# High parts of the recurrence's 16 weight tiles by a casting transfer on GpSimd's queue

## The chip, the cores and the metric

The kernel runs on one core of a Trainium2 chip. The metric is the device time of one execution in microseconds. The median of three runs before the change is 1561.8 us (1561.55 to 1561.82).

## What is computed

A decoder trunk of two layers over 512 positions of width 1024, all in float32. Each layer adds half a feed-forward block, a token mixer, and half a feed-forward block again, each behind a root-mean-square norm. The mixer of layer 0 is a recurrence (RG-LRU behind a causal convolution of width 4), that of layer 1 a chunked spatial gating. The change touches the first product of the recurrence:

```python
def recurrent_mixer(x, w_in, conv_w, conv_b, gate_a_w, gate_a_b, gate_x_w, gate_x_b, lam, w_out):
    y, r = jnp.split(x @ w_in, 2, axis=-1)
    y = jax.nn.gelu(y)
    r = causal_depthwise_conv(r, conv_w, conv_b)
    h = rg_lru(r, gate_a_w, gate_a_b, gate_x_w, gate_x_b, lam)
    return (y * h) @ w_out
```

Here w_in is 1024 x 2048: its right half gives r, its left half y.

## The kernel before

**Splitting.** TensorE multiplies in a rounded 32-bit format (float32r). To keep float32's accuracy, each factor is split in two: hi is the value rounded to float32r, lo is the value minus hi. A product is then three matmuls: high by high, high by low, low by high (mm3, L242). For a weight tile this is done in Sub.split (L189): ScalarE copies the loaded tile raw into whi with the rounding (L202), and VectorE subtracts whi from raw into wlo (L203). All ScalarE activations carry the line of the helper act (L114), all two-tensor operations of VectorE that of tt (L105), and those with a scalar that of stt (L111). So the profile's lines tell helpers, and the tile names tell the work.

**Weight tiles.** A tile is 128 x 1024 float32, 512 KB. SyncE loads it into one of 10 buffers called raw (L153). Some tiles of other stages get a second weight added by GpSimd's accumulating load (L156). The pool wp has 4 buffers for whi and 4 for wlo (L77). There is no such loading for the recurrence's input products beyond the plain load.

**The order of the work** is written out by hand. The kernel is a list of products (subs), and the loop at L1760 goes through it: for product i it first issues the splits up to product i + 3 (SPLIT_AHEAD), then work that was hung on this place by name ("mid", "rest"), then loads, then the matmuls of product i, then what takes their result from PSUM ("end", "late"). Every engine takes its own instructions in the order of issue, and a wait for another engine or for a transfer stops all that is behind it on the same engine.

**The recurrence's input products** (recurrent, mk, L1338) are 16 tiles of 1024 rows by 128 columns, loaded in rows of 512 bytes, each for 24 matmuls. The first eight, r0 to r7, give r; the next eight, y0 to y7, give y. The first four run in two halves over the positions, because the second half of the normed input is ready later: r0 to r3 over the first 256 positions, then a0 to a3 over the other 256 with the same whi and wlo. The others run over all 512 positions at once. Between r2 and r3 TensorE transposes the second half of the normed input (L700).

When the result for block c of r is there, ScalarE takes it from PSUM and VectorE adds the other three taps of the convolution (taps, L1227: three stt into rc). In the next step rc is split (hi on ScalarE, lo<-rc on VectorE), and then TensorE forms two gate products from it (gate, L1231: six matmuls, the second and the fifth of which read lo). In VectorE's order the subtraction for the tile three products ahead stands before that lo<-rc, since splits of weights come first in each step. From block 0 on there stands also a product (pr) between them, once the gates' results come back.

**The stage before** is the output product of the first feed-forward block. Its last four products run just before r0, in 12 matmuls each. In the last of them two splits are called ahead of time and one after it (L837 to L840). In this region VectorE also splits the gates' weights (gw) and updates the sum x, then scales the rows that the transposes before r3 take (xn).

Of the kernel before, what the change touches and what calls it, by code (L numbers as in the profile page):

```python
# [9 lines left out]
F32R = mybir.dt.float32r  # L10
U16 = mybir.dt.uint16
AF = mybir.ActivationFunctionType
ALU = mybir.AluOpType

P = 128
# [55 lines left out]
def trunk(ctx: ExitStack, tc: tile.TileContext, a: dict, out: bass.AP):  # L71
    nc = tc.nc
# [4 lines left out]
    wp = ctx.enter_context(tc.tile_pool(name="wp", bufs=4))  # L77
# [7 lines left out]
    def nm(s):  # L85
        uid[0] += 1
        return f"{s}_{uid[0]}"

    def slot(dt=F32, name="s"):
        return sp.tile([P, T], dt, tag="s", name=nm(name))  # L90
# [10 lines left out]
    def f32(t):  # L101
        return t.bitcast(F32)

    def tt(o, x, y, op):
        nc.vector.tensor_tensor(out=o, in0=x, in1=y, op=op)  # L105
# [7 lines left out]
    def act(o, x, f, **k):  # L113
        nc.scalar.activation(out=o, in_=x, func=f, **k)  # L114

    def split(src):

        w = src.shape[-1]
        hi, lo = slot(F32R, "hi")[:, :w], slot(F32R, "lo")[:, :w]
        act(hi, src, AF.Copy)  # L120
        tt(lo, src, f32(hi), ALU.subtract)
        return hi, lo
# [6 lines left out]
    class Raw:  # L129


        halves = False

        def __init__(self, src, shape, plus=None, wait=2):
            self.src, self.shape, self.plus, self.wait, self.uses, self.done = src, shape, plus, wait, 0, 0
# [19 lines left out]
        def add(self, src):  # L155
            nc.gpsimd.dma_start(out=self.v, in_=src, accum_op=ALU.add)  # L156
# [6 lines left out]
    def run_pending():  # L163
        while pending and pending[0][0] <= now[0]:
            raw = pending.pop(0)[1]
            raw.add(raw.plus)
            raw.plus = None

    class Sub:
# [4 lines left out]
        def __init__(self, raw, mm, post=None, tile=None, then=None, tile_then=None):  # L174
            self.raw, self.mm, self.post, self.tile, self.then = raw, mm, post, tile, then
            self.tile_then = tile_then
            self.hi, self.at = None, (raw.turn(), tile and tile.turn())

        def add(self):
            if self.tile is None or (self.raw.done, self.tile.done) != self.at:  # L180
# [5 lines left out]
            self.tile.used()  # L186
            self.tile = None

        def split(self, between=None):  # L189

            if self.hi is not None:
                return
            self.add()
            src = self.raw.v
            assert self.tile is None and self.raw.plus is None and self.raw.done == self.at[0]
            _, k, c = src.shape
            self.hi = wp.tile([P, 1024], F32R, tag="whi", name=nm("whi"))[:, : k * c].rearrange(
                "p (k c) -> p k c", k=k)
            self.lo = wp.tile([P, 1024], F32R, tag="wlo", name=nm("wlo"))[:, : k * c].rearrange(
                "p (k c) -> p k c", k=k)  # L200
            for q in ((slice(0, 1), slice(1, 2)) if self.raw.halves else (slice(0, k),)):
                act(self.hi[:, q, :], src[:, q, :], AF.Copy)  # L202
                tt(self.lo[:, q, :], src[:, q, :], f32(self.hi[:, q, :]), ALU.subtract)  # L203
                if between is not None and q.start == 0:
                    between()
            if self.then is not None:
                self.raw.add(self.then)
            self.raw.used()

    class Again:  # L210
# [3 lines left out]
            self.sub, self.mm, self.post = sub, lambda _: mm(sub), post  # L214

        def add(self):
            pass

        def split(self):
# [4 lines left out]
    def raw_of(src, shape, *plus):  # L224
        raws.append(Raw(src, shape, *plus))
        return raws[-1]

    subs = []
# [9 lines left out]
    def run(phase):  # L238
        for fn in hooks.pop((now[0], phase), []):
            fn()  # L240

    def mm3(ps, wh, wl, xh, xl, start, stop):  # L242
        nc.tensor.matmul(ps, wh, xh, start=start, stop=False)  # L243
        nc.tensor.matmul(ps, wh, xl, start=False, stop=False)  # L244
        nc.tensor.matmul(ps, wl, xh, start=False, stop=stop)  # L245
# [24 lines left out]
    class Group:  # L270
# [81 lines left out]
        def parts(self, name, last=False):  # L352
            if name in self.gain:
                self.direct(name, self.f[name], [g for g, _ in self.gain[name]])
            else:
                self.hl[name] = split(self.f[name])
            if last:
                del self.f[name]
# [703 lines left out]
    class FinalNorm:  # L1062
# [90 lines left out]
        def keep(self, scale):  # L1153

            n = now[0]

            def parts():
                self.x = split(xt(1, 1))
                self.eye = cp.tile([P, P], F32R, tag="eye", name="eye")
                act(self.eye, ident, AF.Copy, scale=1.0 / scale)  # L1160

            def gain():
                self.gain[2] = slot(name="fg")
                act(self.gain[2], self.gain[1], AF.Copy, scale=scale)

            hook(n + 2, "mid", parts)
            hook(n + 3, "mid", gain)
# [30 lines left out]
    def recurrent(w_in, w_out, norm):  # L1198
# [10 lines left out]
        def split_gate(name, q):  # L1209
            gates[name, q] = split(gates[name, q])  # L1210
# [127 lines left out]
        def mk(c0, post, halves):  # L1338

            raw = raw_of(w_in[:, c0 : c0 + P].rearrange("(k p) c -> p k c", p=P), [P, KD, P])  # L1340
            st = {}

            def mm_of(t):
                def mm(s):
                    if not st:
                        st[0] = (aux if c0 < 2 * P else bank)("r")
                    for k in KORDER:
                        xh, xl = (z[:, t] for z in S.z[k])
                        mm3(st[0][:, t], s.hi[:, k, :], s.lo[:, k, :], xh, xl, k == KORDER[0], k == KORDER[-1])
                return mm  # L1350

            last = lambda: post(st[0])
            if not halves:
                subs.append(Sub(raw, mm_of(slice(0, T)), last))
                return []
            subs.append(Sub(raw, mm_of(slice(0, H))))
            return [Again(subs[-1], mm_of(slice(H, T)), last)]

        again = []
        for c in range(4):  # L1360
            again += mk(D + c * P, lambda ps, c=c: r_post(c, ps), True)
        subs.extend(again)
        for c in range(4, KD):
            mk(D + c * P, lambda ps, c=c: r_post(c, ps), False)
        assert len(subs) == y0
        for c in range(KD):
            mk(c * P, lambda ps, c=c: y_post(c, ps), False)
# [251 lines left out]
    def load_more(n=len(raws)):  # L1619
        nonlocal loaded  # L1620
        while loaded < n and len(live) < RAW_BUFS:
            raws[loaded].load()
            loaded += 1
# [136 lines left out]
    for i, s in enumerate(subs):  # L1760
        now[0] = i
        run_pending()
        run("pre")
        upto = ahead.get(i, i + SPLIT_AHEAD)
        for q in range(i, min(upto + 1, len(subs))):
            if i >= 2 and q == upto and q + 1 < len(subs):
                subs[q + 1].add()
            subs[q].split()
        run("mid")
        run("rest")  # L1770
        load_more()
        s.mm(s)
        run("end")
        if s.post is not None:
            s.post()
        run("late")
# [26 lines left out]
```

## Time and profile before

| | us |
|---|---|
| runs, median (lowest to highest) | 1561.8 (1561.55 to 1561.82) |
| span of the profiled execution, first to last instruction | 1559.5 |
| ScalarE's copies raw to whi, whole kernel: 567, mean 1.001 | 564.4 |
| VectorE's subtractions to wlo, whole kernel: 567, mean 1.153 | 651.9 |
| GpSimd busy | 245.3 |

The page gives the span of the profiled execution and no time of its own beside it; the runs' median is 2.3 us above the span. The granted clock of TensorE is 0.999 on the mean. Windows and timelines below count from the span's start. In the timeline a line has the start, the length, the engine, the source line, the operation, out<-in, and in brackets the idle time before it with what ended it. In the windows, the recurrence's input products stand from 329 to 430 us.

A matmul's length in the timeline (0.39 us for 512 columns) overlaps the next one's: starts are 0.227 us apart for 512 columns and 0.12 for 256.

### The profile page before, as it was taken

Reading aid. Unit: us, or ns where it says so; the run is one execution under the profiler, and the core shown is the slowest. Engines: PE = TensorE matmul, PEld = TensorE weight load, DVE = VectorE, ACT = ScalarE, POOL = GpSimd, SP = SyncE. Lnnn points to the kernel's source line nnn. Section 1 sums busy time; section 2 is a strip of 40 time slices with the busy share of each in tenths; the row PEclk is TensorE's granted clock in tenths of the full one; section 3 lists DMA queues with packets and bytes.
Section 4 is the critical chain, followed back from the end, with each engine's and each line's share of the span. In section 5 each row is a group of like instructions: output and inputs, shape, how many; then the busy total and the mean of one; then the engine's idle time right before and its main releaser. Section 6 shows DMA issues by size and latency. Waiting matters only on the chain.

```text
span 1559.5 us, 21004 instructions
## 1 busy us (share of the span) xinstructions
PE 1551.9 (100%) x7293; PEld 1318.4 (85%) x7293; DVE 1309.5 (84%) x1776; ACT 1188.7 (76%) x1777; POOL 245.3 (16%) x220
## 2 busy tenths in 40 slices
PE   9999999999999999999999999999999999999998
PEld 7888888898888998888889988888888889888886
DVE  6977789888999777789897877798879997777998
ACT  7877787668778868796877787867787877778856
POOL 2111112300020111112211111122211111111220
PEclk9999999999999999999999999999999999999999
DMA  9888899953395988899977888989878859898994
GB/s 315 189 189 196 186 217 229 228 137 109 103 230 137 191 199 198 189 232 224 244 179 183 188 203 185 227 227 238 224 191 219 203 138 216 197 212 177 241 235 138
DMA packets 268763, 310.53 MB, mean 199 GB/s; under 512 B 111232, under 2 KB 149232, under 8 KB 268656
## 3 DMA queue, kind: packets, MB, share of 16 engines
q1 hardware_dynamic: 214368, 210.02, 46.4%
q0 software_dynamic: 52496, 97.33, 37.0%
q10 hardware_dynamic: 1792, 1.84, 0.4%
q8 instruction: 57, 0.93, 0.2%
q14 instruction: 50, 0.41, 0.1%
HBM read 282.39 MB, written 2.10 MB: 182 GB/s over the span
## 4 chain that ended last, share of the span: by engine, by line
PE 98%; DVE 1%; DMA 0%; ACT 0%; issue 0%; SPq 0%; DVEq 0%
PE A L479 15%; PE A L478 15%; PE A L480 15%; PE C L480 8%; PE C L479 8%; PE C L478 8%; PE B L479 4%; PE B L480 4%; PE B L478 4%; PE r L243 2%; PE r L244 2%; PE r L245 2%; PE Q L480 2%; PE Q L479 2%; PE Q L478 2%; PE p L958 1%
## 5 line engine op out<-in xcount | busy, mean ns | idle before, releaser
L105 DVE TENSOR_TENSOR wlo<-raw,whi 128x1024 fp32r<-128x1024 f32 (+2 forms) x567 | 651.9, 1153 | 208.3 <-ACT whi L114 206.7
L114 ACT ACTIVATE whi<-raw 128x1024 fp32r<-128x1024 f32 (+2 forms) x567 | 564.4, 1001 | 239.0 <-DVE raw L105 93.1
L478 PE MATMUL A<-whi,hi 128*128 128x512 f32 (+1 forms) x1104 | 421.0, 381 | 0.0
L479 PE MATMUL A<-whi,lo 128*128 128x512 f32 (+1 forms) x1104 | 419.3, 380 | 0.1
L480 PE MATMUL A<-wlo,hi 128*128 128x512 f32 (+1 forms) x1104 | 419.3, 380 | 0.0
L478 PEld LDWEIGHTS A<-whi,hi 128*128 128x128 f32 x1104 | 207.3, 188 | 35.9 <-ACT c L114 1.0
L480 PEld LDWEIGHTS A<-wlo,hi 128*128 128x128 f32 x1104 | 207.2, 188 | 35.6
L479 PEld LDWEIGHTS A<-whi,lo 128*128 128x128 f32 x1104 | 207.3, 188 | 35.4 <-DVE lo L105 0.5
L156 POOL DMA_DIRECT2D raw<-in_ffn_w_in_dram x100 | 120.7, 1207 | 710.1 <-DVE raw L105 322.8
L478 PE MATMUL C<-whi,hi 128*128 128x512 f32 (+1 forms) x608 | 231.4, 381 | 0.0
L479 PE MATMUL C<-whi,lo 128*128 128x512 f32 (+1 forms) x608 | 231.3, 380 | 0.0
L480 PE MATMUL C<-wlo,hi 128*128 128x512 f32 (+1 forms) x608 | 231.3, 380 | 0.0
L156 POOL DMA_DIRECT2D raw<-in_ffn_w_out_dram x73 | 83.8, 1194 | 319.1 <-DVE wlo L105 199.2
L105 DVE TENSOR_TENSOR raw<-raw,raw 128x1024 f32<-128x1024 f32 (+1 forms) x113 | 131.0, 1159 | 1.1
L479 PEld LDWEIGHTS C<-whi,lo 128*128 128x128 f32 x608 | 114.1, 188 | 20.1 <-DVE lo L105 0.2
L478 PEld LDWEIGHTS C<-whi,hi 128*128 128x128 f32 x608 | 114.2, 188 | 19.9
L480 PEld LDWEIGHTS C<-wlo,hi 128*128 128x128 f32 x608 | 114.1, 188 | 19.9
L105 DVE TENSOR_TENSOR lo<-a,hi 128x512 fp32r<-128x512 f32 (+1 forms) x184 | 119.7, 658 | 1.4 <-ACT hi L114 1.3
L114 ACT ACTIVATE hi<-a 128x512 fp32r<-128x512 f32 (+1 forms) x184 | 107.8, 596 | 14.5 <-DVE a L105 12.8
L114 ACT ACTIVATE c<-A 128x512 f32<-128x512 f32 (+1 forms) x150 | 81.9, 567 | 46.5 <-PE A L480 46.1
L479 PE MATMUL B<-whi,lo 128*128 128x512 f32 (+1 forms) x304 | 115.7, 381 | 0.2 <-DVE lo L111 0.2
L478 PE MATMUL B<-whi,hi 128*128 128x512 f32 (+1 forms) x304 | 115.7, 381 | 0.0
(189 smaller groups left out, 1964.5 us busy)
## 6 DMA issues: line engine op xcount, KB each, us to landing
raw<-in_ffn_w_in_dram SPq DMA_DIRECT2D x143, 512.0 KB, 5.6
raw<-in_ffn_w_out_dram SPq DMA_DIRECT2D x98, 512.0 KB, 5.7
raw<-in_ffn_w_in_dram POOLq DMA_DIRECT2D x76, 512.0 KB, 7.7
raw<-in_ffn_w_out_dram POOLq DMA_DIRECT2D x58, 512.0 KB, 7.6
raw<-in_ffn_w_in_dram SPq DMA_DIRECT2D x48, 384.0 KB, 4.2
raw<-in_sg_w_in_dram SPq DMA_DIRECT2D x20, 512.0 KB, 7.0
raw<-in_ffn_w_in_dram POOLq DMA_DIRECT2D x24, 384.0 KB, 6.3
raw<-in_rec_w_in_dram SPq DMA_DIRECT2D x16, 512.0 KB, 5.4
```

What stands on the lines that cost most here:

```text
L105: nc.vector.tensor_tensor(out=o, in0=x, in1=y, op=op)
L114: nc.scalar.activation(out=o, in_=x, func=f, **k)
L156: nc.gpsimd.dma_start(out=self.v, in_=src, accum_op=ALU.add)
L243: nc.tensor.matmul(ps, wh, xh, start=start, stop=False)
L244: nc.tensor.matmul(ps, wh, xl, start=False, stop=False)
L245: nc.tensor.matmul(ps, wl, xh, start=False, stop=stop)
L478: nc.tensor.matmul(ps, zh, wh, start=fresh and i == 0, stop=False, **k)
L479: nc.tensor.matmul(ps, zl, wh, start=False, stop=False, **k)
L480: nc.tensor.matmul(ps, zh, wl, start=False, stop=end, **k)
L958: nc.tensor.matmul(bank_of(half, s), z, (sub.lo if m == 2 else sub.hi)[:, q, :], start=left[2] == "2" and (h, q, m) == (0, 0, 0), stop=lef ...
```

## The change

The 16 tiles of mk are marked (raw.cast = True). For a marked tile, whi is no longer written by ScalarE's copy: a second transfer reads the same weights from DRAM again and writes them into whi, converting float32 to float32r on the way. It is issued by GpSimd's queue. The loop issues it for the product one beyond the splits, that is four ahead, after the splits of this step and ahead of this product's matmuls. VectorE's subtraction stays where it was. The plain load of raw stays as well, since the subtraction reads it. If the transfer was not issued ahead, split issues it itself.

```diff
@@ class Raw
-        halves = False
+        halves = cast = False
@@ class Sub
+        def cast(self):
+
+            if not self.raw.cast or self.hi is not None:
+                return
+            _, k, c = self.raw.v.shape
+            self.hi = wp.tile([P, 1024], F32R, tag="whi", name=nm("whi"))[:, : k * c].rearrange(
+                "p (k c) -> p k c", k=k)
+            nc.gpsimd.dma_start(out=self.hi, in_=self.raw.src)
+
         def split(self, between=None):
 
+            if self.raw.cast and self.lo is None:
+                self.cast()
+                _, k, c = self.raw.v.shape
+                self.lo = wp.tile([P, 1024], F32R, tag="wlo", name=nm("wlo"))[:, : k * c].rearrange(
+                    "p (k c) -> p k c", k=k)
+                tt(self.lo, self.raw.v, f32(self.hi), ALU.subtract)
+                self.raw.used()
             if self.hi is not None:
                 return
@@ def mk
             raw = raw_of(w_in[:, c0 : c0 + P].rearrange("(k p) c -> p k c", p=P), [P, KD, P])
+            raw.cast = True
@@ the loop over subs
             subs[q].split()
+        if upto + 1 < len(subs):
+            subs[upto + 1].cast()
         run("mid")
```

More of the change, by code (lines that the diff above doesn't have):

```diff
@@ L176, in __init__ @@
             self.tile_then = tile_then
-            self.hi, self.at = None, (raw.turn(), tile and tile.turn())
+            self.hi, self.lo, self.at = None, None, (raw.turn(), tile and tile.turn())
         def add(self):
@@ L216, in add, with cast @@
         def add(self):
+            pass
+        def cast(self):
             pass
```

## The prediction

> **What bounds the kernel now.** I read the page's first and fourth part, then TensorE's waits over the whole span, then the windows of the recurrence's input products.
>
> ```profile
> span 1559.5 us, 21004 instructions
> PE 1551.9 (100%) x7293; PEld 1318.4 (85%) x7293; DVE 1309.5 (84%) x1776; ACT 1188.7 (76%) x1777; POOL 245.3 (16%) x220
> PE 98%; DVE 1%; DMA 0%; ACT 0%; issue 0%; SPq 0%; DVEq 0%
> ```
>
> ```profile
> PE warm L1640 <- DVE warm L1635: 1.3, 1, 1.3
> PE B L479 <- DVE lo L111: 0.2, 1, 0.2
> ```
>
> ```profile
> 345.13:392.00 46.87, 46.87 (x243) 40.11 (x241) 39.99 (x53) 38.66 (x54) 2.41 (x2) 1.00 0.37 98
> 392.00:430.00 38.00, 38.00 (x169) 31.50 (x168) 36.53 (x52) 27.18 (x38) 3.12 (x3) 1.00 0.36 102
> ```
>
> The reader is to see three things. TensorE bounds everything: 1551.9 of 1559.5 us, 98% of the chain that ended last, and in the whole span it waited 1.5 us for others. In the two windows (length; busy us of PE, PEld, DVE, ACT, POOL; clock; DMA share; GB/s) it has no idle time at all. VectorE is nearly as full there, 85% and then 96%. So nothing that becomes cheaper on ScalarE can bring time, and whatever makes TensorE wait is paid in full, because no later stage has slack on TensorE to win it back.
>
> **What goes.** ScalarE's copies raw to whi of the 16 tiles, each like the one at 346.01 below, 1.05 us: 16.8 us of ScalarE. They lie beside TensorE's matmuls, so they are worth 0 to the end. VectorE's subtraction no longer waits for ScalarE.
>
> **What comes.** Sixteen casting transfers on GpSimd's queue, 512 KB each, and a new wait. The whi ring has 4 buffers. When the transfer for the product four ahead is called for, all four belong to this product and the next three, so the transfer waits until TensorE has ended this product. Before, the copy waited for the same buffer, but took 1.05 us. Now the subtraction that makes wlo, in its old place in VectorE's order, waits for release, issue and landing. Behind it on VectorE stand the low parts of the convolved rows (lo<-rc), and TensorE's gate products wait for those.
>
> **How long the transfer takes** (D, issue to landing). No casting transfer is in this trace, so it is bounded by neighbours of the same 512 KB, all in the stretch after 348 us. The first fence has GpSimd's accumulating loads issued at 387.64 and at 367.08 (last column: us to landing), the second their issues, the third SyncE's plain loads of the very same weights in rows of 512 bytes.
>
> ```profile
> raw<-in_rec_w_out_dram POOLq DMA_DIRECT2D x1, 512.0 KB, 6.1
> raw<-in_rec_w_out_dram POOLq DMA_DIRECT2D x1, 512.0 KB, 8.2
> ```
>
> ```profile
> 367.08 1.21 POOL L156 DMA_DIRECT2D raw<-in_rec_w_out_dram  x1 [59.97 <-DMA raw<-in_rec_w_out_dram]
> 387.64 1.20 POOL L156 DMA_DIRECT2D raw<-in_rec_w_out_dram  x1 [19.35 <-DMA raw<-in_rec_w_out_dram]
> ```
>
> ```profile
> DMA to landing us min/median/max: 3.9/3.9/3.9
> ```
>
> ```profile
> 420.08 1.23 DVE L105 TENSOR_TENSOR wlo<-raw,whi 128x1024 fp32r<-128x1024 f32 x1 [0.26 <-ACT whi L114]
> 421.62 1.20 POOL L156 DMA_DIRECT2D raw<-in_rec_w_out_dram  x1 [32.78 <-DVE wlo L105]
> ```
>
> ```profile
> L156 POOL DMA_DIRECT2D raw<-in_rec_w_out_dram x8 | 9.7, 1268 | 132.2 <-DMA raw<-in_rec_w_out_dram 79.3 <-DVE wlo L105 52.8
> L1653 POOL DMA_DIRECT2D stage<-in_rec_lambda_dram x1 | 0.5, 499 | 4.0 <-DMA raw<-in_ffn_w_in_dram 4.0
> q0 software_dynamic: 52496, 97.33, 37.0%
> ```
>
> (The last line, the software queue's packets, MB and share of 16 engines, serves a rival below.) From the end of the releasing instruction (420.08 + 1.23) to the issue on GpSimd go 0.3 us. Low end of D: 3.9, if a cast is as quick as SyncE's plain load. A cast does not read its destination as an accumulation does, which speaks for less than 6.1. But it has rows of 512 bytes: 1024 where an accumulating load of 2048-byte rows has 256. GpSimd's instruction takes 0.50 us for 4 KB in 8 rows and 1.27 for 256 rows, 0.003 us a row; 1024 rows would then take about 3.6 us (an estimate), which speaks for more. I take D = 6.1, the calm accumulating load: same queue, same bytes, same stretch. High end within reason: 8.2 to 9.
>
> The Trainium skill speaks against this size: "DMA: Bandwidth & Descriptors", section "Anatomy of one DMA — SWDGE (gpsimd) path", fits a transfer on this path as 2.0 us plus its bytes at 436 GB/s, by which 512 KB would land in 3.2 us. The trace does not agree for its own transfers on that queue (6.1 and 8.2 us); by the rule the sum below would be 0, which is the first rival.
>
> **Where TensorE will wait.** A product's matmuls follow each other without a gap, so its end is the next one's first matmul plus about 0.16 us. Names: r0 to r7 and y0 to y7 are the 16 tiles in order, a0 to a3 the second halves of r0 to r3.
>
> Place 1, gate(0). TensorE's and VectorE's rows, and ScalarE's copy:
>
> ```profile
> 345.13 0.28 PE L243 MATMUL r<-zh,whi 128*128 128x256 f32 x1
> 351.12 0.40 PE L244 MATMUL gate<-lo,hi 128*128 128x512 f32 x1
> ```
>
> ```profile
> 346.01 1.05 ACT L114 ACTIVATE whi<-raw 128x1024 fp32r<-128x1024 f32 x1
> ```
>
> ```profile
> 346.14 2.32 DVE L111 SCALAR_TENSOR_TENSOR rc<-r,vec,rc 128x509 f32<-128x509 f32 x3 [2.78 <-ACT rc L114]
> 348.38 1.22 DVE L105 TENSOR_TENSOR wlo<-raw,whi 128x1024 fp32r<-128x1024 f32 x1
> 349.51 0.68 DVE L105 TENSOR_TENSOR lo<-rc,hi 128x512 fp32r<-128x512 f32 x1
> ```
>
> 345.13 is a1's first matmul, so a0 and with it r0's whi buffer are done at 345.3. r4's transfer is issued at 345.6 and lands at 351.7. VectorE, ready at 348.4, stands until then; subtraction 1.13 (start to start), lo<-rc 0.69: 353.5. The second gate matmul needs that lo and would have run at 351.12. **Wait 2.4 us.** In general the wait is 0.46 + D + 1.13 + 0.69 less the 5.99 us between those two matmuls: it opens at D = 3.7.
>
> Places 2 and 3, gate(4) and gate(7). Here a product of 0.60 (pr<-rc,g) stands between subtraction and lo:
>
> ```profile
> 362.08 0.39 PE L243 MATMUL gate<-hi,hi 128*128 128x512 f32 x1
> 370.46 0.39 PE L244 MATMUL gate<-lo,hi 128*128 128x512 f32 x1
> 383.84 0.39 PE L243 MATMUL r<-zh,whi 128*128 128x512 f32 x1
> 390.86 0.39 PE L244 MATMUL gate<-lo,hi 128*128 128x512 f32 x1
> ```
>
> ```profile
> 387.62 1.21 DVE L105 TENSOR_TENSOR wlo<-raw,whi 128x1024 fp32r<-128x1024 f32 x1
> 388.75 0.69 DVE L105 TENSOR_TENSOR pr<-rc,g 128x512 f32<-128x512 f32 x1
> 389.35 0.68 DVE L105 TENSOR_TENSOR lo<-rc,hi 128x512 fp32r<-128x512 f32 x1
> ```
>
> From the buffer's release to a low part in use go 0.46 + 6.1 + 1.13 + 0.60 + 0.69 = 8.98 us. For gate(4) the product r4 ends before 362.08 and the low part is wanted at 370.46, 8.38 later: **wait 0.6**. For gate(7) r7 ends before 383.84 and it is wanted at 390.86, 7.02 later: **wait 2.0**. They open at D = 5.5 and 4.1. Gates 1, 2, 3, 5 and 6 have a longer way or gain it from the wait before them: 0.
>
> Place 4, r2. The first tiles' transfers wait for the FFN's last four output products, 12 matmuls and 2.72 us each; the second of them ends before 323.56, so the others before 320.84, 326.28 and 329.00:
>
> ```profile
> 323.56 0.39 PE L478 MATMUL A<-whi,hi 128*128 128x512 f32 x1
> 335.00 0.28 PE L245 MATMUL r<-zh,wlo 128*128 128x256 f32 x1
> 339.30 0.36 PE L243 MATMUL r<-zh,whi 128*128 128x256 f32 x1
> ```
>
> ```profile
> 325.07 0.68 DVE L105 TENSOR_TENSOR lo<-gw,hi 128x512 fp32r<-128x512 f32 x1
> 325.67 1.22 DVE L105 TENSOR_TENSOR wlo<-raw,whi 128x1024 fp32r<-128x1024 f32 x1
> 326.81 0.68 DVE L105 TENSOR_TENSOR lo<-gw,hi 128x512 fp32r<-128x512 f32 x1
> 327.41 2.48 DVE L111 SCALAR_TENSOR_TENSOR x<-A,x 128x512 f32<-128x512 f32 x4
> 329.80 1.27 DVE L111 SCALAR_TENSOR_TENSOR x<-Q,x 128x512 f32<-128x512 f32 x2
> 331.00 1.21 DVE L105 TENSOR_TENSOR wlo<-raw,whi 128x1024 fp32r<-128x1024 f32 x1
> ```
>
> r1's tile lands at 323.56 + 0.46 + 6.1 = 330.1, and VectorE, which began that subtraction at 325.67, now stands for it. Then 1.14 + 0.60 + 2.4 + 1.2 and r2's subtraction 1.13 with 0.1 to be seen: 336.7. r2's first matmul on wlo ran at 335.00. **Wait 1.7**, opening at D = 4.4. r0's own low part is there at 328.5 and TensorE wants it at 329.2: 0, but at D above 6.8 it too is late.
>
> **Sum:** 2.4 + 0.6 + 2.0 + 1.7 = 6.7 us; 1559.5 + 6.7 = 1566.2 in the profiled execution's own span. The runs' median of 1561.8 lies 2.3 above the span, what lies around it, and I keep that: **1568.5 us**.
>
> **Costed at nothing.** After gate(7) VectorE is about as late as TensorE, so the y products find their wlo in time. r3's transfer is only called for inside its own split; it is due at 335.6 and read by TensorE from 339.30. The DMA engines are 36 to 37% busy, and 16 more transfers of 512 KB hide there; without that cover D rises, which the range holds. On GpSimd's queue two of the gates' memsets now come behind r2's transfer, issued at 326.7; the gate weights loaded into them are split only after r3. Two of the accumulating loads stand between the transfers, but wait for loads that land before the next buffer is free: 0, and if one blocked, D would grow for one tile. PSUM: if r4's bank is the one that the third convolution's rows free, r4 waits up to 0.8 more; taken as 0, held in the range.
>
> **The rivals.**
> 1. Not slower: the transfer lands fast. Place: the same four waits; point of decision: D. At D = 5.1 they are 1.4 + 0 + 1.0 + 0.7 = 3.1 us; at 3.9 only gate(0)'s 0.2 are left. Time 1562 to 1564.9. For it: SyncE's plain load of the same rows at 3.9. Against: every load of GpSimd's in that stretch.
> 2. Much slower: a packet of the cast costs what an accumulating one does. 37.0% of 1559.5 us on 16 engines over 52496 packets is 0.176 us each; 64 rows for each engine make 11.3 us, D about 12, and the four waits and r0's make some 30 us: 1592. At D = 9 it is 18 us, 1580. For it: four times the rows. Against: a cast reads nothing back.
> 3. The change does not do what it says: the transfer copies bits and rounds nothing. Then its time is the forecast's still, and only the values differ. The Trainium skill, same page, section "SWDGE vs HWDGE vs iDMA", says that a float32r destination always casts and only from GpSimd; no run here shows it, and it moves no term.
> 4. Faster: ScalarE's 16.8 us would have to shorten a wait of TensorE's, and it has 1.5 us of those in the whole span, none in this stage.
>
> **How the numbers follow.** Forecast (D from 5.1 to 9, 1565 to 1580): 0.62. Rival 1: 0.22. Rival 2 above D = 9: 0.12. Rival 4: 0.04. Rival 3 has no time of its own. About 0.2%, 3.1 us, is what a measurement of this kernel can tell from no change. Slower 0.62 + 0.12 = 0.74, same 0.22, faster 0.04. Range: 1562 (D under 4) to 1582 (D near 10), which leaves out some 1 in 10 on either side.
>
> **What would show it.** In the changed trace the transfer's time to landing is the one number to read first. Right: TensorE's waits name VectorE's lo at L105 at the second matmul of gate(0) and gate(7), some 2 us each, and VectorE's name the DMA of whi. Wrong: TensorE without idle time between 329 and 392, or waits at wlo inside the y products, or a transfer issued long before or after the end of the product whose buffer it takes.

## The result: 10 us slower, and the profile after

| | before | after |
|---|---|---|
| runs, median (lowest to highest), us | 1561.81 (1561.55 to 1563.87) | 1571.87 (1570.97 to 1572.77) |
| span of the profiled execution, us | 1559.5 | 1571.0 |
| profiled execution's own time, us | not given | 1572.77 |

The ratio is 1.0063, with a 95% interval from 1.0051 to 1.0075. The forecast was +6.7 us and 1568.5; measured is +10.1 us by the medians and +11.5 by the two spans, which compare one execution each. Of the four executions after, two took 1572.7 us at a mean granted clock of 0.998, the profiled one among them, and two 1571.0 us at 0.999; so what the views below show of a half clock may hold for the first pair alone. In the changed kernel the lines behind the new code have moved: mm3 by 19 to L262 to L264, the warm-up by 20 to L1660. The casting transfer is L196.

The same views after, page first, then TensorE's waits (line, whom it waited for, us in total, times, longest):

```profile
span 1571.0 us, 21027 instructions
PE 1555.5 (99%) x7293; PEld 1319.1 (84%) x7293; DVE 1309.6 (83%) x1776; ACT 1173.7 (75%) x1761; POOL 257.5 (16%) x236
...
q0 software_dynamic: 69136, 105.72, 39.6%
...
PE 93%; issue 3%; DVE 2%; DMA 1%; ACT 1%; POOL 0%; SPq 0%; POOLq 0%; DVEq 0%; ACTq 0%
```

```profile
PE gate L263 <- DVE lo L105: 3.8, 4, 1.4
PE r L264 <- DVE wlo L105: 3.0, 2, 2.2
PE warm L1660 <- DVE warm L1655: 1.3, 1, 1.3
PE r L262 <- DMA whi<-in_rec_w_in_dram: 1.0, 1, 1.0
```

ScalarE has its 16 instructions less and 15.0 us less work (1188.7 to 1173.7), and the time does not show it. TensorE, which waited 1.5 us in the whole span before, now waits 7.8 us more in three new kinds: at gate products for VectorE's lo, inside r products for wlo, and once for a transfer itself. Each of them in TensorE's timeline (in brackets the wait and its releaser):

```profile
333.33 0.36 PE L262 MATMUL r<-zh,whi 128*128 128x256 f32 x1 [1.03 <-DMA whi<-in_rec_w_in_dram]
334.67 0.39 PE L264 MATMUL r<-zh,wlo 128*128 128x256 f32 x1 [0.86 <-DVE wlo L105]
339.99 0.58 PE L264 MATMUL r<-zh,wlo 128*128 128x256 f32 x1 [2.18 <-DVE wlo L105]
...
359.25 0.50 PE L263 MATMUL gate<-lo,hi 128*128 128x512 f32 x1 [1.45 <-DVE lo L105]
379.38 0.50 PE L263 MATMUL gate<-lo,hi 128*128 128x512 f32 x1 [0.36 <-DVE lo L105]
387.20 0.50 PE L263 MATMUL gate<-lo,hi 128*128 128x512 f32 x1 [0.73 <-DVE lo L105]
402.32 0.50 PE L263 MATMUL gate<-lo,hi 128*128 128x512 f32 x1 [1.22 <-DVE lo L105]
```

In order these are r1 (twice), r2, gate(0), gate(4), gate(5) and gate(7). The cause of one of them, gate(0), on GpSimd and VectorE:

```profile
351.99 0.88 POOL L196 DMA_DIRECT2D whi<-in_rec_w_in_dram  x1 [21.62 <-PE r L264]
```

```profile
352.73 2.31 DVE L111 SCALAR_TENSOR_TENSOR rc<-r,vec,rc 128x509 f32<-128x509 f32 x3 [2.84 <-ACT rc L114]
357.37 1.23 DVE L105 TENSOR_TENSOR wlo<-raw,whi 128x1024 fp32r<-128x1024 f32 x1 [2.33 <-DMA whi<-in_rec_w_in_dram]
358.51 0.69 DVE L105 TENSOR_TENSOR lo<-rc,hi 128x512 fp32r<-128x512 f32 x1
```

The reader is to see the chain: GpSimd waits for the end of a product (PE r L264) and issues; VectorE has its convolution done at 355.0, stands 2.33 us for the landing, subtracts, and only then makes the lo that TensorE has been waiting for. The subtraction's own tile, r4, is not wanted before 364.87. What is late is only what stands behind it.

Landing times of the casting transfers, from the list of DMA issues (all 16 with their median, then single ones from short windows: r1, r4, y0 and y1), and their spread from the view of the line that issues them:

```profile
whi<-in_rec_w_in_dram POOLq DMA_DIRECT2D x16, 512.0 KB, 5.6
whi<-in_rec_w_in_dram POOLq DMA_DIRECT2D x1, 512.0 KB, 9.1
whi<-in_rec_w_in_dram POOLq DMA_DIRECT2D x1, 512.0 KB, 5.4
whi<-in_rec_w_in_dram POOLq DMA_DIRECT2D x1, 512.0 KB, 6.1
whi<-in_rec_w_in_dram POOLq DMA_DIRECT2D x1, 512.0 KB, 7.1
```

```profile
DMA to landing us min/median/max: 4.5/5.6/9.1
```

And two windows of the changed kernel (length; busy of PE, PEld, DVE, ACT, POOL; granted clock; DMA share; GB/s), then the first of them before the change:

```profile
324.00:333.50 9.50, 8.47 (x49) 7.36 (x49) 2.21 (x4) 0.05 (x1) 3.63 (x5) 1.00 1.27 250
340.20:343.20 3.00, 3.00 (x15) 3.00 (x16) 2.56 (x10) 0.93 (x2) 0.00 (x0) 0.50 0.66 177
```

```profile
324.00:333.50 9.50, 9.50 (x61) 8.62 (x60) 9.09 (x18) 5.52 (x13) 0.00 (x0) 1.00 0.76 197
```

While the transfers of r1 to r3 fly, the DMA engines' share is 1.27 (transfers overlap in it) where it was 0.76, and VectorE works 2.21 of 9.5 us where it worked 9.09. Right behind the wait at r2 the granted clock is 0.50 for three microseconds.

### The profile page after: what moved, and what is told of

The parts are those of the page before. It is cut to its first block, busy times and chain, and to the rows that moved or that the text cites. A ratio compares the mean times of both kernels' runs of the same rounds, so it can differ in the third digit from the quotient of the medians.

```text
span 1571.0 us, 21027 instructions
## 1 busy us (share of the span) xinstructions
PE 1555.5 (99%) x7293; PEld 1319.1 (84%) x7293; DVE 1309.6 (83%) x1776; ACT 1173.7 (75%) x1761; POOL 257.5 (16%) x236
## 3 DMA queue, kind: packets, MB, share of 16 engines
q0 software_dynamic: 69136, 105.72, 39.6%
## 4 chain that ended last, share of the span: by engine, by line
PE 93%; issue 3%; DVE 2%; DMA 1%; ACT 1%; POOL 0%; SPq 0%; POOLq 0%; DVEq 0%; ACTq 0%
PE A L498 15%; PE A L499 15%; PE A L497 15%; PE C L499 8%; PE C L498 8%; PE C L497 8%; PE B L498 4%; PE B L499 4%; PE B L497 4%; PE Q L499 1%; PE Q L498 1%; PE Q L497 1%; PE p L977 1%; PE e L308 1%; PE r L262 1%
## 5 line engine op out<-in xcount | busy, mean ns | idle before, releaser
L114 ACT ACTIVATE whi<-raw 128x1024 fp32r<-128x1024 f32 (+2 forms) x551 | 547.7, 1000 | 239.2 <-DVE raw L105 94.8
```

## The experiments

The theory (A): TensorE loses what VectorE, in its fixed order, stands for a landing that begins only when a whi buffer is free. The main rival (B): the cost is the extra traffic, or the casting transfer and its use as such. Every ratio is to the kernel before, run beside it.

| run | median, us | ratio (95% interval) |
|---|---|---|
| e1_rest | 1566.27 | 1.0029 (1.0019 to 1.0038) |
| e2_first4 | 1567.29 | 1.0029 (1.0020 to 1.0039) |
| e3_traffic | 1562.77 | 1.0002 (0.9991 to 1.0013) |
| e5_lateslo | 1568.23 | 1.0034 (1.0024 to 1.0045) |
| e4_ring5 | 1562.52 | 1.0002 (0.9993 to 1.0011) |
| e6_noahead | 1573.62 | 1.0072 (1.0055 to 1.0089) |
| e7_r1only | 1563.35 | 1.0013 (1.0004 to 1.0022) |
| e8_ring5_rest | 1561.22 | 0.9995 (0.9985 to 1.0004) |

The kernel before had medians of 1561.59 beside the first four and 1561.73 beside the others.

**1. One part of the tiles alone.**

```diff
-            raw.cast = True
+            raw.cast = not D <= c0 < D + 4 * P     # e1_rest
+            raw.cast = D <= c0 < D + 4 * P         # e2_first4
```

> Casting transfers for r4 to r7 and y0 to y7 only; r0 to r3 are copied by ScalarE as before. Theory A (VectorE stands in order for the landing, and TensorE then for the low part at a gate): the waits at gate(0), (4), (5) and (7) stay, 1.6 + 0.5 + 0.9 + 1.4 in the changed trace, so +4 to +5 us over the kernel before, and nothing is lost ahead of a0. Theory B (the cost is the extra DMA traffic, spread over the transfers): 12 of 16 transfers, so three quarters of +10, +7.5 us, with later landings of other loads.

> Casting transfers for r0 to r3 only, ScalarE copies for the other 12 tiles. Theory A: the waits at r1 and r2 stay with their slow matmuls behind r2's wait, +5 to +6.5 us, and no wait at any gate; with the run that has only the other 12 it adds up to the whole +10. Theory B: a quarter of the traffic, +2.5 us.

Measured: +4.7 and +5.7 us by the medians; by the ratios' centres 4.5 us each, and 9.1 together, against 9.8 for the change. For e1_rest both figures are in A's range; for e2_first4 the medians are, and the ratio's centre lies 0.5 us below it. B's +7.5 for twelve tiles is out of the first interval (3.0 to 5.9 us); B's +2.5 for four is out of the second (3.1 to 6.1). TensorE's waits are where A has them, in e1_rest and in e2_first4:

```profile
PE gate L263 <- DVE lo L105: 4.6, 4, 1.7
```

```profile
PE r L264 <- DVE wlo L105: 3.0, 2, 2.2
PE r L262 <- DMA whi<-in_rec_w_in_dram: 0.6, 1, 0.6
```

So four tiles of sixteen cost as much as the other twelve.

**2. The traffic alone.** (In part: SLOTS is 55 too, and the split of a marked tile goes back to ScalarE's copy.)

```diff
+            copy = wp.tile([P, 1024], F32R, tag="copy", name=nm("copy"), bufs=1)[:, : k * c].rearrange(
+                "p (k c) -> p k c", k=k)
+            nc.gpsimd.dma_start(out=copy, in_=self.raw.src)
```

> The kernel before, ScalarE copies and all, plus the 16 casting transfers at the same places of the program into one tile that nothing reads (one slot of 2 KB less in the slot pool to make room). The ring of the tile has one buffer, so each transfer only waits for the one before. Theory A: within 0.2% of the kernel before, 1560 to 1564 us, as nobody waits for a landing. Theory B: most of the +10 us is there.

Measured: 1562.77 us, no difference that the interval tells. In its trace TensorE waits for nothing but its warm-up, though the DMA share from 321 to 327 us is 1.65, against 0.94 in the change:

```profile
321.00:327.00 6.00, 6.00 (x28) 4.98 (x27) 6.00 (x10) 4.75 (x8) 1.41 (x2) 1.00 1.65 292
```

B falls as far as traffic goes: 8.4 MB more cost no more than 2 us by the upper end of the interval, as long as nobody stands for them. The transfers here come one after the other, so this run has the bytes of the change and not its crowd of three casting transfers at once.

**3. A fifth buffer, which frees each buffer one product earlier.** (In part: the ring of the tiles that ScalarE copies gets the same bufs=5, and e8_ring5_rest has e1_rest's line besides.)

```diff
-SLOTS = 56
+SLOTS = 55
-            self.hi = wp.tile([P, 1024], F32R, tag="whi", name=nm("whi"))[:, : k * c].rearrange(
+            self.hi = wp.tile([P, 1024], F32R, tag="whi", name=nm("whi"), bufs=5)[:, : k * c].rearrange(
```

> The change with a ring of 5 buffers for whi in place of 4 (one slot of 2 KB less in the slot pool). Each transfer's buffer is then free one product earlier. Theory A: release to want grows by 5.4 to 6.9 us at the gates, more than the 0.5 to 1.7 us that was waited there, so no gate waits any more. Ahead of r0 the buffers come free 2.7 us earlier each, so r1 lands near 330 and the waits at r1 and r2 shrink to 0 to 2 us. In all 1562 to 1565 us. A theory that the cast itself, or a subtraction that reads what a transfer wrote, is slow would leave it near 1572.

> A ring of 5 buffers for whi, casting transfers for r4 to r7 and y0 to y7 only. Theory A: no wait of TensorE's is left, so the time of the kernel before within 0.2%, 1560 to 1564 us; and not less, because ScalarE's 12 copies that are gone stood beside TensorE's work.

Measured: 1562.52 and 1561.22 us, neither to be told from the kernel before. In e4_ring5 no gate waits any more; r2 still waits 0.8 us. A wait of 1.2 us that I had not expected stands at 1035.70 us, in the output product of the third feed-forward block, 600 us behind the last casting transfer:

```profile
PE C L498 <- DVE lo L105: 1.2, 1, 1.2
PE r L264 <- DVE wlo L105: 0.8, 1, 0.8
```

The same wait comes back in e5_lateslo and e6_noahead, and not in the change; why is open. The transfers are no quicker here (median 6.4 us, r1's 8.1, r4's 12.2), they only start earlier. So the cast as such is not the price; the time from release to want is. e8_ring5_rest also shows what the change brings without its waits: 12 copies taken off ScalarE, no wait in the recurrence (a single new one of 0.4 us stands at 1519 us, in the last feed-forward block), and no time won. The fifth buffer without any casting transfer was not run; in the kernel before it could save TensorE little, since 0.2 us is all that it waits there besides its warm-up.

**4. The subtraction one product later.**

```diff
         for q in range(i, min(upto + 1, len(subs))):
+            if q > i + 2 and isinstance(subs[q], Sub) and subs[q].raw.cast:
+                continue
```

> All 16 casting transfers, issued where they were, but VectorE's subtraction for a cast tile is called one product later (two products ahead of use and not three; r2's, which is called by a hook, stays). Theory A: the landing is over when VectorE gets there, so the waits at the gates go (about 4 to 5 us less than the change), and what is lost at r1 and r2, where the transfer itself lands late, largely stays: +2 to +6 us over the kernel before. Theory B: as long as the change, +10 us.

Measured: 1568.23 us, 6.6 us over the kernel before by the medians and 5.3 by the ratio of 1.0034, at the upper end of what A expected or just above it, and not in the way that A expected. The gates' waits are gone, all four. Others have come:

```profile
PE r L264 <- DVE wlo L105: 3.5, 4, 2.1
PE C L498 <- DVE lo L105: 1.2, 1, 1.2
PE r L262 <- DMA whi<-in_rec_w_in_dram: 0.7, 1, 0.7
PE A L498 <- DVE lo L105: 0.4, 1, 0.4
```

```profile
419.58 0.80 PE L264 MATMUL r<-zh,wlo 128*128 128x512 f32 x1 [2.13 <-DVE wlo L105]
```

That is a y product. From 392 on VectorE is busy nearly without a pause (36.7 of 38 us; scans and products of the recurrence), so it comes to the postponed subtraction too late. By TensorE's start times this wait and the half clock behind it cost 4.0 us, while r1 and r2 lose only 2.6 us here, against 6.3 in the change. So A missed twice: less was left at r1 and r2, and a y product lost what had been free. The waits at C and A are those of the third feed-forward block, at 1040 and 1043 us. One order fits the r products, the other the y products.

**5. Does the place of the call count?**

```diff
-        if upto + 1 < len(subs):
-            subs[upto + 1].cast()
```

> The change without the call that issues the transfer ahead: the transfer is issued inside split, one product later in the program. Theory A: the buffer's release sets the issue and not the place of the call, and the release is the same, so the time is the change's, 1570 to 1574 us. If the place of the call counted, each landing would be a product (5.4 us) later and the waits larger by as much, 1585 us or more.

Measured: 1573.62 us. The issue times stay tied to the ends of the same products; the call ahead did nothing of use, because four buffers hold it back. It lies 1.8 us above the change's median, and the intervals of the two ratios overlap; its longest wait is 2.9 us at gate(5), for y1's transfer, which was issued 2.1 us behind an accumulating load and took 9.1 us to land:

```profile
387.40 0.50 PE L263 MATMUL gate<-lo,hi 128*128 128x512 f32 x1 [2.92 <-DVE lo L105]
```

```profile
whi<-in_rec_w_in_dram POOLq DMA_DIRECT2D x1, 512.0 KB, 9.1
raw<-in_rec_w_out_dram POOLq DMA_DIRECT2D x1, 512.0 KB, 5.9
```


**6. One transfer alone.**

```diff
-            raw.cast = True
+            raw.cast = c0 == D + P
```

> A casting transfer for r1 alone, all other tiles copied by ScalarE. In the change r1's transfer took 9.1 us to land. If it is slow because three casting transfers and the plain loads run together there, it lands in 5 to 7 us now, r1 does not wait for it, r2's low part is some 1 us late: +0 to +2 us, 1562 to 1563.6. If the plain loads alone make it slow it still takes about 9, and the waits at r1 and r2 stay: +4 to +6 us.

Measured: 1563.35 us; r1's transfer lands in 6.2 us instead of 9.1, r1 does not wait, r2 waits 1.3:

```profile
whi<-in_rec_w_in_dram POOLq DMA_DIRECT2D x1, 512.0 KB, 6.2
```

```profile
PE r L264 <- DVE wlo L105: 1.3, 1, 1.3
```

So the 9.1 us need several casting transfers in flight. Beside r1's transfer flew one plain load of a raw tile here, which landed in 4.1 us; in the change it was one such load, which took 8.4 us, and the casting transfers of r0, r2 and r3.

## Why the prediction was right, and where it was short

The sign, the mechanism and the four places forecast (r2 and three gates) held, two more came; the sum was short by a third (6.7 of 10.1 us by the medians, and of 11.6 in the profiled execution, which the table gives). Each place's cost is read as the change of TensorE's start times across it, after against before:

| place | forecast, us | measured, us | landing D, forecast 6.1 |
|---|---|---|---|
| r1 | 0 | 2.4 | 9.1 |
| r2 and the slow clock behind it | 1.7 | 3.9 | (r1's) |
| gate(0) | 2.4 | 1.7 | 5.4 |
| gate(4) | 0.6 | 0.7 | 6.1 |
| gate(5) | 0 | 1.0 | 7.1 |
| gate(7) | 2.0 | 1.5 | 5.6 |
| shifts of about 0.1 each, and 0.3 ahead of r0 | 0 | 0.4 | |
| sum | 6.7 | 11.6 | |

- **What bounds the kernel**: right. Nothing that TensorE lost was won back later, its last recurrence product starts 11.6 us later and the span is 11.5 longer. ScalarE's relief was worth 0 (e8_ring5_rest).
- **The gates**: right, with the formula too. With each tile's own D in place of 6.1 it gives 1.7, 0.6, 0.9 and 1.5 for the four gates, against 1.7, 0.7, 1.0 and 1.5. That the sum of 5.0 forecast is 4.9 measured is luck: an overestimate at gate(0) and gate(7) and the miss of gate(5) cancel. Gate(5) was put at 0 because at D = 6.1 it just closes; y1's transfer, for which VectorE stood, took 7.1.
- **The step that failed is the size of D for the first tiles.** It was taken from an accumulating load in the calm stretch after 348 us and used also for r1 to r3, which fly from 324 to 339 with each other and with the plain loads. There D is 9.0 to 9.1 (e7_r1only: 6.2 for one alone). This made r1 wait, for which the forecast has no term, and took r2 to 2.2. The prediction had said that contention raises D and had left it to the range. But its "36 to 37% busy" was read from 345 us on; from 324 to 333.5 the share was 0.76 before the change, as shown above. And its 3.9 and 6.1 us were the calm end of what the kernel before showed. Over the whole span its plain loads of these same tiles, and the accumulating loads of the feed-forward blocks' first weights, are these:

```profile
DMA to landing us min/median/max: 3.9/5.4/9.1
```

```profile
raw<-in_ffn_w_in_dram POOLq DMA_DIRECT2D x76, 512.0 KB, 7.7
```

- **From span to time**: the 2.3 us that the prediction added are too many by some 0.6. The executions before that list both have 1.65 to 1.76 us between span and time. With 1.7 the forecast would have been 1567.9.
- **Not foreseen**: the granted clock of 0.50 behind r2, worth about 1.4 us in the profiled execution (13 matmuls at 0.213 us where they take 0.12, and the first step after the wait).
- **GpSimd's time for rows**: wrong. The estimate of 3.6 us for 1024 rows stands against 0.87 to 0.93 us measured. It did not enter the sum.
- **Rivals.** The fast landing did not come: 4.5 us at the quickest, for y4 to y6, where no wait opened. The much slower one neither: the 16 transfers added 16640 packets and 45 us of 16 engines' time (39.6% of 1571.0 less 37.0% of 1559.5), 0.043 us a packet against 0.176 for the queue's packets before. The Trainium skill's fit ("DMA: Bandwidth & Descriptors", section "Anatomy of one DMA — SWDGE (gpsimd) path") would give 3.2 us, an estimate; the trace's 4.5 to 9.1 does not agree, and by the fit no wait would have opened.
- **Costed at nothing**: the memsets on GpSimd did move behind r2's transfer, and no wait of TensorE's leads to them. The bank for r4 cost no visible wait. That the y products find their wlo in time held in the change, and failed in e5_lateslo.

## What to carry to other kernels

Here a copy of one microsecond on an engine with time to spare could not be replaced for free by a transfer of 4.5 to 9: if both must wait for the same buffer, the reader stands for the difference, and on an engine with a fixed order everything behind the reader stands too. Before moving such a step, work out the time from the buffer's release to the first thing that is wanted behind the reader; give the transfer a buffer that is free that much earlier, and size its landing from a stretch that is as crowded as its own. And where one engine is busy for the whole span, relief for another is worth nothing: the best version here only came back to the time of the kernel before.

## What the runs showed of the hardware

A casting load from float32 to float32r in rows of 512 bytes costs GpSimd 0.9 us and lands in 4.4 us in the quietest case (e4_ring5), close to SyncE's plain load of the same rows (3.9), and in 9 us where several overlap, up to 12.2 in e4_ring5.

TensorE's granted clock fell to about half for some 3 us after waits of 2.2 us at r2 in the change and in e2_first4, and after one of 2.1 us in e5_lateslo, whose window right behind that wait is this:

```profile
419.80:423.20 3.40, 3.40 (x9) 2.69 (x10) 3.04 (x7) 1.12 (x2) 0.00 (x0) 0.53 0.47 154
```

It fell in e6_noahead too, and there behind the two waits at r1, of 1.1 and 0.9 us: from 334.8 to 338.0 us its matmuls of 256 columns start 0.21 us apart in place of 0.12. In the change two waits of nearly the same length stand at the same place (1.03 and 0.86 us), and the clock stays whole behind them. A window behind r1's waits in e6_noahead, then one in the change:

```profile
336.00:339.70 3.70, 3.06 (x18) 2.85 (x17) 3.70 (x7) 2.28 (x8) 0.00 (x0) 0.72 0.88 210
335.00:337.50 2.50, 2.50 (x23) 2.50 (x22) 2.50 (x5) 1.34 (x4) 0.00 (x0) 1.00 1.01 229
```

Nor did it fall behind the longest wait of all, 2.9 us at gate(5) in e6_noahead, whose window behind it is this:

```profile
389.00:392.00 3.00, 3.00 (x15) 2.48 (x14) 2.89 (x5) 1.17 (x2) 0.00 (x0) 1.00 0.26 98
```

So the length of a wait alone does not decide it. The Trainium skill ("TensorE: Matmul & The Clock Gate", section "Part 1: The HAM clock gate") has a monitor that looks at activity in free-running windows of 3.4 us and halves the clock after an idle one, by which the position of the wait in the window would matter. The half clock and its length agree with that. The idle window does not: no wait of TensorE's here fills 3.4 us, and waits of 1.1 and 0.9 us were enough in e6_noahead. That the position decides was not tried.
